# A down-projection by Strassen's seven products instead of eight block products

## The chip, the cores and the metric

The kernel runs on one core of one Trainium2 chip. The metric is the device time of one execution in microseconds. The core has five engines that work side by side, each with its own queue in a fixed order: TensorE (PE, matmuls into PSUM), VectorE (DVE) and GpSimd (POOL) for elementwise work, ScalarE (ACT) for activations and copies, and SyncE (SP), which here issues nearly all transfers. The kernel is written in Tile, which traces the program, lays out each engine's queue by a timeline of its own, and places the semaphores. Only blocks under `in_order` have the order of the named engines fixed by hand.

## The reference

One layer of a sequence model on x of 512 tokens by 1024 channels, all in float32: a token-mixing sublayer (two branches, merged and projected), then a gated MLP. The change is in the MLP, which is this, with D_FF = 2752 and ALPHA = 2 ** 0.25:

```python
x = layer_norm(ALPHA * x + merged @ w_out[l], ln1_g[l], ln1_b[l])
u = causal_dwconv(x @ w_up[l], f_conv_w[l], f_conv_b[l])      # width 3
u_gate, u_val = jnp.split(u, 2, -1)
x = layer_norm(ALPHA * x + (jax.nn.silu(u_gate) * u_val) @ w_down[l], ln2_g[l], ln2_b[l])
```

## The kernel before

**Products in three matmuls.** Every float32 operand is split into a high part H, rounded to the PE's `fp32r` format by a copy on ACT, and a low part L, the source minus H, on DVE. A product is then H·H + L·H + H·L: three matmuls of 128x128 stationary against 512 moving columns, added up in a PSUM bank.

**The weight stream.** The weights lie in HBM as a list of units, 128 partitions by 1024 numbers each (512 KB), in the order in which they are used (`unit_list`). `advance` (L132) loads a unit (L136) up to four ahead into one of three `raw` tiles, and splits it up to two ahead into one of three pairs `wH`, `wL` (L159, L165). The loads wait in SP's queue for a free `raw` tile, and the splits for a free pair.

**The MLP.** 21 full tiles of 128 features and one half tile of 64. For each full tile, `feature_major` multiplies the gate unit (UG) and the value unit (UV), 24 matmuls each, with features on the partitions and the 512 tokens along the columns. Then ACT and DVE apply the convolution's taps (L505, L507), SiLU (L1050), the product of gate and value (L1051), and the split into `fH` and `fL` (L1053, L1054). The half tiles of gate and value come together in one unit (UM), and their product is put as H on 64 partitions and as L on the other 64 of one tile, `fHm` (L1061 to L1066), so that two matmuls do the work of three.

**The residual.** x after the first LayerNorm went to HBM as `x1d` without its gamma and beta. While the MLP ends, SP loads gammas and betas (L914) and the eight half rows `x1r` (L1076), and DVE folds gamma and beta in, sixteen operations of 128x512 (L1077, L1078). Their tiles come free as the last up-projection reads the old inputs for the last time.

**The down-projection.** `wide_product` multiplies token-major: four token tiles of 128 by two halves of 512 output channels, in the eight PSUM banks at once. It goes through the units of `w_down` one after another, 24 matmuls a unit, `step` (L944). The last five units (half tile included) are multiplied bank by bank, so that the banks are done one after another and each token tile's residual sum (L1090), statistics (L1091), normalisation and store go on beside the next bank's matmuls. This end is in a fixed order on PE, DVE, ACT and POOL: the rsqrt of LayerNorm (L232) and the addition of the last beta (L1109) are on POOL, the shift and scale on ACT (L1115), the multiplication by gamma on DVE (L1108).

Of the kernel before, what the change touches and what calls it, by code (L numbers as in the profile page):

```python
# [87 lines left out]
def trunk(ctx, tc, x, wts, pcm, prow, out):  # L88
# [10 lines left out]
    def mm_bank(name):  # L99
        return pm.tile([P, 512], F32, tag="mm", name=name)  # L100
# [29 lines left out]
    EXTRA.update({u: ("ff", "xw", "xw", 4) for u in UX["DN"][-2:]})  # L130

    def advance(n, hl=HL_AHEAD):  # L132
        while st["raw"] <= min(n + RAW_AHEAD, len(UNITS) - 1):
# [5 lines left out]
        while st["hl"] <= min(n + hl, len(UNITS) - 1):  # L139
# [5 lines left out]
            if u == UX["DN"][-3]:  # L145
                hls[u] = [[tmp(f"w{q}{u}{i}", F32R) for i in range(2)] for q in "HL"]
                for i in range(2):
                    r_ = raw[:, 512 * i:512 * i + 512]
                    nc.scalar.copy(hls[u][0][i], r_)
                    nc.vector.tensor_tensor(hls[u][1][i], r_, hls[u][0][i].bitcast(F32), ALU.subtract)  # L150
                st["hl"] += 1
                continue
            H = pool.tile([P, 1024], F32R, tag=tH, name=f"wH{u}", bufs=nb_)
            L = pool.tile([P, 1024], F32R, tag=tL, name=f"wL{u}", bufs=nb_)
            if u == 0:
                nc.gpsimd.tensor_copy(H[:, 0:512], raw[:, 0:512])
                nc.scalar.copy(H[:, 512:], raw[:, 512:])
            else:
                nc.scalar.copy(H, raw)  # L159
            if u == len(UNITS) - 1:  # L160
                nc.gpsimd.memset(L[64:128, :].bitcast(F32), 0.0)
                nc.vector.tensor_tensor(L[0:64, :], raw[0:64, :], H[0:64, :].bitcast(F32), ALU.subtract)
            else:
                eng = nc.gpsimd if u == 0 else nc.vector
                eng.tensor_tensor(L, raw, H.bitcast(F32), ALU.subtract)  # L165
# [28 lines left out]
    def tmp(name, dt=F32, shape=(P, 512)):  # L194
        return tp.tile(list(shape), dt, tag="tmp", name=name)
# [865 lines left out]
    nc.scalar.activation(tg[0:64, :], tg[0:64, :], AF.Silu)  # L1061
    nc.scalar.copy(tv[0:64, :], tg[64:128, :])
    nc.vector.tensor_tensor(tg[0:64, :], tg[0:64, :], tv[0:64, :], ALU.mult)
    H = hpart("fHm")
    nc.scalar.copy(H[0:64, :], tg[0:64, :])
    nc.vector.tensor_tensor(H[64:128, :], tg[0:64, :], H[0:64, :].bitcast(F32), ALU.subtract)  # L1066
# [20 lines left out]
    def wd(c, hf):
        ps = wd_tail(c, hf)
        rr = x1r[c][hf]
        nc.vector.scalar_tensor_tensor(rr, rr, ALPHA, ps, ALU.mult, ALU.add)  # L1090
        nc.vector.bn_stats(bn2[c][:, hf, :], rr)  # L1091
        if hf == 1:
            ln_finish(bn2[c], mv2[:, c, :], rs2[:, c:c + 1], f"2_{c}")

    def store(c, hf, n0=0, n1=512):
        nc.sync.dma_start(out[c * P:(c + 1) * P, 512 * hf + n0:512 * hf + n1], x1r[c][hf][:, n0:n1])

    def shift(c):
        nb = cst.tile([P, 1], F32, tag="nb", name=f"nb2_{c}", bufs=4)
        nc.vector.scalar_tensor_tensor(nb, mv2[:, c, 0:1], -1.0, rs2[:, c:c + 1], ALU.mult, ALU.mult)  # L1100
        return nb

    with in_order(*CORE):
        for c in range(NC):
            wd(c, 0)
            if c > 0:
                for hf in range(2):
                    nc.vector.tensor_tensor(x1r[c - 1][hf], x1r[c - 1][hf], gt2[0][hf], ALU.mult)  # L1108
                    nc.gpsimd.tensor_tensor(x1r[c - 1][hf], x1r[c - 1][hf], gt2[1][hf], ALU.add)  # L1109
                    store(c - 1, hf)  # L1110
            wd(c, 1)
            nb = shift(c)
            if c < NC - 1:
                for hf in range(2):
                    nc.scalar.activation(x1r[c][hf], x1r[c][hf], AF.Identity, bias=nb, scale=rs2[:, c:c + 1])  # L1115
# [84 lines left out]
```

## Time and profile before

| what | value |
|---|---|
| median of 3 runs | 942.77 us (942.12 to 942.94) |
| the profiled execution | 942.7 us, of which the span is 941.0 us |
| PE busy | 924.0 us, 98% of the span |
| DVE busy | 555.0 us, 59% |
| ACT busy | 382.3 us, 41% |
| POOL busy | 66.0 us, 7% |
| up-projection | to 812.7 us |
| down-projection's matmuls | 812.7 to 931.8 us |
| end | 931.8 to 941.0 us |

A row of the groups gives line, engine, operation, the tile written and the tiles read, shapes and count; then busy time and the mean duration in ns; then idle time ahead of them and what ended it. A row of a timeline gives start and length in us, and in brackets the idle time of its engine just before and what released it. A row of the chain gives start and length of a piece of the sequence of waits that ended last. Matmuls overlap one another, so the length of one is more than the distance to the next.

### The profile page before, as it was taken

The numbers are of one execution on the slowest core, as the hardware profiler recorded it, in microseconds if no ns is written. First come the engines' busy times: TensorE is split into PE (matmuls) and PEld (weight loads), VectorE is DVE, ScalarE is ACT, GpSimd is POOL, SyncE is SP. The second block draws the span as 40 slices with busy tenths as digits, with TensorE's granted clock in tenths as the row PEclk, the third lists the DMA queues.
The fourth block names the chain that finished last, engine by engine and source line by source line (L and its number), as shares of the span: only waits on it lengthen the run. The fifth ranks groups of instructions, "written<-read, shape, count | busy, mean of one in ns | idle before, by whom it ended". The sixth has DMA issues, their size and how long they took to land.

```text
span 941.0 us, 11703 instructions
## 1 busy us (share of the span) xinstructions
PE 924.0 (98%) x4565; PEld 762.3 (81%) x4565; DVE 555.0 (59%) x916; ACT 382.3 (41%) x572; POOL 66.0 (7%) x81
## 2 busy tenths in 40 slices
PE   7999999999999999999999999999999999999996
PEld 4988888888877888888888888888888888878884
DVE  6685889873556465324339467666666556642246
ACT  4456456442664552234122235544444444332121
POOL 3000000211012510000000000000000000000005
PEclk8999999999999999999999999999999999999998
DMA  5334326453232432223334352222322322632212
GB/s 186 105 101 138 109 88 142 123 147 118 90 111 70 139 109 77 102 90 96 106 112 157 112 178 91 90 90 92 109 90 93 110 90 91 251 128 90 95 62 90
DMA packets 46311, 105.13 MB, mean 112 GB/s; under 512 B 4064, under 2 KB 21144, under 8 KB 46256
## 3 DMA queue, kind: packets, MB, share of 16 engines
q1 hardware_dynamic: 45456, 103.30, 34.0%
q0 software_dynamic: 512, 1.07, 0.4%
q8 instruction: 36, 0.59, 0.3%
q14 instruction: 19, 0.16, 0.1%
q10 hardware_dynamic: 288, 0.02, 0.0%
HBM read 100.08 MB, written 4.30 MB: 111 GB/s over the span
## 4 chain that ended last, share of the span: by engine, by line
PE 94%; DVE 2%; DMA 1%; issue 1%; POOL 0%; ACT 0%; DVEq 0%; ACTq 0%; POOLq 0%
PE u L185 23%; PE wd L944 10%; PE g L185 9%; PE z L185 5%; PE o L185 5%; PE v L575 5%; PE xs L185 5%; PE pb L185 5%; PE pa L185 5%; PE wo L944 4%; PE bc L185 4%; PE q L185 2%; PE k L185 2%; PE bc L335 1%; PE up L185 1%
## 5 line engine op out<-in xcount | busy, mean ns | idle before, releaser
L165 DVE TENSOR_TENSOR wL<-raw,wH 128x1024 fp32r<-128x1024 f32 x151 | 186.4, 1238 | 231.3 <-ACT wH L159 229.2
L159 ACT CAST wH<-raw 128x1024 fp32r<-128x1024 f32 x152 | 159.1, 1051 | 285.5 <-PE g L185 62.8
L185 PE MATMUL u<-x1H,wL 128*128 128x512 f32 x312 | 121.4, 389 | 0.0
L185 PE MATMUL u<-x1L,wH 128*128 128x512 f32 x312 | 121.4, 389 | 0.0
L185 PE MATMUL u<-x1H,wH 128*128 128x512 f32 x312 | 121.4, 389 | 0.0
L185 PEld LDWEIGHTS u<-x1H,wH 128*128 128x128 f32 x312 | 58.6, 188 | 12.1
L185 PEld LDWEIGHTS u<-x1H,wL 128*128 128x128 f32 x312 | 58.6, 188 | 12.0
L185 PEld LDWEIGHTS u<-x1L,wH 128*128 128x128 f32 x312 | 58.6, 188 | 11.8
L944 PE MATMUL wd<-wH,fH 128*128 128x512 f32 x168 | 65.5, 390 | 0.8 <-ACT wH L159 0.8
L944 PE MATMUL wd<-wH,fL 128*128 128x512 f32 x168 | 65.4, 389 | 0.0
L944 PE MATMUL wd<-wL,fH 128*128 128x512 f32 x168 | 63.9, 389 | 0.0
L185 PE MATMUL g<-xnH,wH 128*128 128x512 f32 x128 | 50.1, 392 | 0.0
L185 PE MATMUL g<-xnH,wL 128*128 128x512 f32 x128 | 49.8, 389 | 0.0
L185 PE MATMUL g<-xnL,wH 128*128 128x512 f32 x128 | 49.8, 389 | 0.0
L232 POOL TENSOR_TENSOR rs<-ve,mhalf 128x1 f32<-128x1 f32 x12 | 7.6, 629 | 555.8 <-DVE ve L256 555.5
L944 PEld LDWEIGHTS wd<-wH,fH 128*128 128x128 f32 x168 | 31.5, 188 | 7.7 <-ACT wH L159 1.2
L944 PEld LDWEIGHTS wd<-wH,fL 128*128 128x128 f32 x168 | 31.5, 188 | 6.6
L944 PEld LDWEIGHTS wd<-wL,fH 128*128 128x128 f32 x168 | 31.5, 188 | 6.5
L1053 ACT CAST fH<-cg 128x512 fp32r<-128x512 f32 x21 | 13.0, 620 | 53.0 <-DVE cg L1051 53.0
L507 DVE SCALAR_TENSOR_TENSOR cv<-u,par,cv 128x511 f32<-128x511 f32 (+1 forms) x40 | 29.8, 746 | 0.7
L1050 ACT ACTIVATE cg<-cg 128x512 f32<-128x512 f32 x21 | 13.3, 632 | 40.8 <-DVE cg L507 40.8
L507 DVE SCALAR_TENSOR_TENSOR cg<-u,par,cg 128x511 f32<-128x511 f32 (+1 forms) x38 | 28.4, 746 | 0.6
(326 smaller groups left out, 1972.2 us busy)
## 6 DMA issues: line engine op xcount, KB each, us to landing
raw<-in_wts_dram SPq DMA_DIRECT2D x154, 512.0 KB, 3.3
csb<-scr SPq DMA_DIRECT2D x8, 512.0 KB, 7.3
gt<-in_prow_dram SPq DMA_DIRECT2D x12, 256.0 KB, 4.7
xt<-in_x_dram SPq DMA_DIRECT2D x4, 512.0 KB, 6.5
rb<-scr SPq DMA_DIRECT2D x4, 512.0 KB, 5.5
res<-in_x_dram SPq DMA_DIRECT2D x4, 512.0 KB, 5.3
x1d<-res SPq DMA_DIRECT2D x4, 512.0 KB, 2.6
x1r<-x1d SPq DMA_DIRECT2D x8, 256.0 KB, 5.7
```

The costliest lines, as they stand in the source:

```text
L159: nc.scalar.copy(H, raw)
L165: eng.tensor_tensor(L, raw, H.bitcast(F32), ALU.subtract)
L185: nc.tensor.matmul(ps[:, t0:t1], w_[:, k, :], a_[k][:, t0:t1], start=i == 0, stop=i == 3 * KD - 1)
L232: nc.gpsimd.tensor_tensor(dst, var, epsl[:, :n], ALU.pow)
L335: nc.tensor.matmul(fb[u][:, t], w_[:, k, :], a_[k][:, t], start=n == 1, stop=n == 3 * KD)
L507: nc.vector.scalar_tensor_tensor(dst[:, d:], ps[:, 0:T - d], prm(ws[n - 1 - d], j)[rows], dst[:, d:], ALU.mult, ALU.add)
L575: nc.tensor.matmul(banks[c], a_[k][:, cs_], w_[:, kk, :], start=first and s == 0, stop=last and s == 2)
L944: nc.tensor.matmul(banks[c, hf], a_[:, cs_], w_, start=k == 0 and s == 0, stop=k == n - 1 and s == len(prs) - 1)
L1050: nc.scalar.activation(tg, tg, AF.Silu)
L1053: nc.scalar.copy(H, tg)
```

## The change

The first 20 feature tiles (2560 rows of `w_down`) are multiplied by Strassen's method in Winograd's form. The features A are cut into quarters, token half by tiles 0 to 9 and 10 to 19, and the weights B likewise, tiles 0 to 9 and 10 to 19 by halves of the output channels:

- S1 = A21 + A22, S2 = S1 - A11, S3 = A11 - A21, S4 = A12 - S2
- T1 = B12 - B11, T2 = B22 - T1, T3 = T2 - B11, T4 = T2 - B21
- seven products: 1 = A11·B11, 2 = A12·B21, 3 = S4·B22, 4 = A22·T4 (made with the other sign), 5 = S1·T1, 6 = S2·T2, 7 = S3·T3

Each product goes over ten feature tiles in five steps of two tiles, for two token tiles, 12 matmuls a step. The order is product 2, 1, 5, then 6 and 3 mixed, 7, and 4. Feature tile 20 and the half tile ("the rest") are multiplied as before, four quarters of ten matmuls each, and ahead of the products.

- The up-projection makes tile i and tile i + 10 one after the other (`UP_ORDER`). POOL adds S1, S2 and S3 for the pair, and the features are split into the parts that the products read directly.
- The stream of units ends with the two units of the rest (DR). The seven products have a stream of their own, 30 blocks of 512 KB: some quarters are loaded more than once.
- The weight sums are made in place, two operations a step for products 5, 6, 7 and 4, on POOL (in product 4 the second one on DVE). Then come the splits on ACT and DVE. Each of the 20 steps of products 5, 6, 7 and 3 also splits a tile of feature sums, and S4 takes one operation of POOL and one of DVE in each step of product 5.
- The results are added to the residual by DVE from PSUM, in several passes: eight scalings with the rest (or product 2) and fourteen additions.
- PE's order is fixed for the whole stage. The order of all four engines is fixed only at the end, where the last two steps of product 4 are made for token tile 2 and then for token tile 3.

The diff, cut to its core:

```diff
-    for j in range(21):
+UP_ORDER = [j for i in range(10) for j in (i, i + 10)] + [20]
+    for j in UP_ORDER:
         add("UG", "cols", "w_up", 128 * j)
         add("UV", "cols", "w_up", FF + 128 * j)
     add("UM", "mixed")
-    for k in range(21):
+    add("DR", "rows", "w_down", 128 * 20)
+    add("DR", "last")
+    for k in range(20):
         add("DN", "rows", "w_down", 128 * k)
-    add("DN", "last")
...
+    for i, j in enumerate(UP_ORDER):
+        tg = gated(i, j)
+        if j < 10:
+            low = tg
+            split(a11[j // 2][0][:, j % 2, :], a11[j // 2][1][:, j % 2, :], tg[:, 0:TH])
+        elif j < 20:
+            p, q = (j - 10) // 2, j % 2
+            split(a2[p][0][:, q, :], a2[p][1][:, q, :], tg)
+            s1, s2, s3 = (sums[p][:, n, q, :] for n in range(3))
+            nc.gpsimd.tensor_tensor(s1, low[:, TH:], tg[:, TH:], ALU.add)
+            nc.gpsimd.tensor_tensor(s2, s1, low[:, 0:TH], ALU.subtract)
+            nc.gpsimd.tensor_tensor(s3, low[:, 0:TH], low[:, TH:], ALU.subtract)
+        else:
+            split(fr[0], fr[1], tg)
...
+    LOAD = {2: (bY, 10, 0), 1: (bX, 0, 0), 5: (bZ, 0, 1), 6: (bX, 10, 1), 3: (bZ, None, None), 7: (bX, 0, 0), 4: (bW, 10, 0)}
+    SUM = {5: 0, 6: 1, 7: 2, 3: 0}
+    steps = ([(2, i) for i in range(5)] + [(1, i) for i in range(5)] + [(5, i) for i in range(5)]
+             + [(6, 0), (6, 1), (3, 0), (6, 2), (3, 1), (6, 3), (3, 2), (6, 4), (3, 3), (3, 4)]
+             + [(7, i) for i in range(5)] + [(4, i) for i in range(5)])
...
+    def split_step(p, i):
+        H = wp.tile([P, 2, 512], F32R, tag="wH", name=f"dnH{p}{i}")
+        L = wp.tile([P, 2, 512], F32R, tag="wL", name=f"dnL{p}{i}")
+        whl[p, i] = H, L
+        if p in (2, 3):
+            raw = blk[(6 if p == 3 else p), i]
+            split(H, L, raw)
+            return
+        for q in range(2):
+            t = tt[2 * i + q]
+            if p in (5, 6, 4):
+                eng = nc.vector if p == 4 and q else nc.gpsimd
+                eng.tensor_tensor(t, blk[p, i][:, q, :], t, ALU.subtract)
+            elif p == 7:
+                nc.gpsimd.tensor_tensor(blk[7, i][:, q, :], t, blk[7, i][:, q, :], ALU.subtract)
+        if p == 7:
+            split(H, L, blk[7, i])
+        else:
+            for q in range(2):
+                split(H[:, q, :], L[:, q, :], tt[2 * i + q])
+
+    def sum_step(p, i):
+        if p in (5, 6, 7, 3):
+            n = at_["srn"]
+            at_["srn"] += 1
+            H, L = sr[2 * (n % 2)], sr[2 * (n % 2) + 1]
+            split(H, L, sums[i][:, SUM[p], :, :])
+            shl[p, i] = H, L
+        if p == 5:
+            s4, a12 = sums[i][:, 0, :, :], [t[:, :, 0:TH].bitcast(F32) for t in a2[i]]
+            nc.gpsimd.tensor_tensor(s4, a12[0], sums[i][:, 1, :, :], ALU.subtract)
+            nc.vector.tensor_tensor(s4, s4, a12[1], ALU.add)
+
+    def ahead(n):
+        for what, f, m in (("load", load_step, n + 3), ("hl", split_step, n + 2), ("s", sum_step, n + 1)):
...
+    def product(p, i, ms=(0, 1)):
+        aH, aL = operand(p, i)
+        H, L = whl[p, i]
+        first = i == 0 and p in (1, 5, 4)
+        for q in range(2):
+            for m in ms:
+                for s_, (a_, w_) in enumerate(((aH, H), (aL, H), (aH, L))):
+                    nc.tensor.matmul(LOAD[p][0][m], a_[:, q, m * P:(m + 1) * P], w_[:, q, :],
...
+    def rest(bank, c0, hf, name):
+        for m in range(2):
...
+            prs = ((fr[0], H0), (fr[1], H0), (fr[0], L0), (fr[2], H1), (fr[2], L1))
...
+    with in_order(ET.PE):
+        rest(bY, 0, 0, "11")
+        rest(bW, 0, 1, "12")
+        scaled(bW, 0, 1)
+        rest(bZ, 2, 1, "22")
+        scaled(bZ, 2, 1)
+        rest(bX, 2, 0, "21")
+        scaled(bX, 2, 0)
+        for n, (p, i) in enumerate(steps[:-2]):
+            ahead(n)
+            product(p, i)
+            if (p, i) == (2, 4):
+                scaled(bY, 0, 0)
...
+            elif p == 7 and i < 2:
+                apply2(i)
+            elif (p, i) == (7, 4):
+                plus(bX, 2, 1)
+                plus(bX, 2, 0)
+                for c in (2, 3):
+                    nc.vector.bn_stats(bn2[c][:, 1, :], x1r[c][1])
+        ahead(len(steps) - 1)
     with in_order(*CORE):
+        for c in (2, 3):
+            for p, i in steps[-2:]:
+                product(p, i, (c - 2,))
+            plus(bW, 2, 0, (c - 2,))
+            nc.vector.bn_stats(bn2[c][:, 0, :], x1r[c][0])
+            ln_finish(bn2[c], mv2[:, c, :], rs2[:, c:c + 1], f"2_{c}")
+            if c == 2:
+                apply2(c)
+        nb = shift(c)
```

`split(H, L, t)` is the ACT copy into H and the DVE subtraction into L. `apply2(c)` is, for one token tile, the shift, two ACT passes, two DVE multiplications, two POOL additions and the stores. The pairs `wH`, `wL` keep their three buffers, and the residual's folds stay where they were in the program, behind the half tile's features and ahead of the down-projection.

More of the change, by code (lines that the diff above doesn't have):

```diff
@@ L129, in trunk @@
     EXTRA[UX["UG"][1]] = ("at", "bc", "bc", 3)
-    EXTRA.update({u: ("ff", "xw", "xw", 4) for u in UX["DN"][-2:]})
+    STREAM_END = UX["DR"][1]
     def advance(n, hl=HL_AHEAD):
-        while st["raw"] <= min(n + RAW_AHEAD, len(UNITS) - 1):
+        while st["raw"] <= min(n + RAW_AHEAD, STREAM_END):
             u = st["raw"]
@@ L1032, in trunk, with gated @@
     FM = [f"fmw{i}" for i in range(3)]
-    def hpart(name):
-        return ff.tile([P, T], F32R, tag="hT", name=name, bufs=43)
-    for j in range(21):
+    TH = T // 2
+    a11 = [[ff.tile([P, 2, TH], F32R, tag="a11", name=f"a11{q}{i}", bufs=10) for q in "HL"] for i in range(5)]
+    a2 = [[ff.tile([P, 2, T], F32R, tag="a2", name=f"a2{q}{i}", bufs=10) for q in "HL"] for i in range(5)]
+    sums = [ff.tile([P, 3, 2, TH], F32, tag="sum", name=f"sum{i}", bufs=5) for i in range(5)]
+    fr = [ff.tile([P, T], F32R, tag="fr", name=f"fr{i}", bufs=3) for i in range(3)]
+    def gated(i, j):
         pgv = []
-        for u in (UX["UG"][j], UX["UV"][j]):
+        for u in (UX["UG"][i], UX["UV"][i]):
             if u in up_banks:
@@ L1082, in trunk @@
     rs2 = cst.tile([P, NC], F32, name="rs2")
-    wd_tail = wide_product(UX["DN"], fH, fL, 5, "wd", last_stack=True)
     bn2 = [bn_tile(f"2_{c}") for c in range(NC)]
[L1087 to L1091, printed above, removed]
+    bX, bY = ([mm_bank(f"wd{n}{i}") for i in range(2)] for n in "xy")
+    bZ, bW = ([sm_bank(f"wd{n}{i}") for i in range(2)] for n in "zw")
@@ new lines, in trunk, with block @@
+    sr = [rp.tile([P, 2, TH], F32R, tag="r", name=f"sr{i}") for i in range(4)]
+    tt = [tmp(f"tt{k}") if k < 8 else ff.tile([P, 512], F32, tag="tt", name=f"tt{k}", bufs=2) for k in range(10)]
+    DN = UX["DN"]
+    def block(k0, hf, i):
+        return wts[DN[k0 + 2 * i]:DN[k0 + 2 * i] + 2, :, 512 * hf:512 * hf + 512].rearrange("u p c -> p u c")
+    LOAD = {2: (bY, 10, 0), 1: (bX, 0, 0), 5: (bZ, 0, 1), 6: (bX, 10, 1), 3: (bZ, None, None), 7: (bX, 0, 0), 4: (bW, 10, 0)}
+    SUM = {5: 0, 6: 1, 7: 2, 3: 0}
@@ new lines, in ahead, with operand @@
+    def ahead(n):
+        for what, f, m in (("load", load_step, n + 3), ("hl", split_step, n + 2), ("s", sum_step, n + 1)):
+            while at_[what] <= min(m, len(steps) - 1):
+                f(*steps[at_[what]])
+                at_[what] += 1
+    def operand(p, i):
+        if p == 1:
+            return [t for t in a11[i]]
+        if p in (2, 4):
+            o = TH * (p == 4)
+            return [t[:, :, o:o + TH] for t in a2[i]]
+        return shl[p, i]
+    def product(p, i, ms=(0, 1)):
+        aH, aL = operand(p, i)
+        H, L = whl[p, i]
+        first = i == 0 and p in (1, 5, 4)
+        for q in range(2):
+            for m in ms:
+                for s_, (a_, w_) in enumerate(((aH, H), (aL, H), (aH, L))):
+                    nc.tensor.matmul(LOAD[p][0][m], a_[:, q, m * P:(m + 1) * P], w_[:, q, :],
+                                     start=first and q == 0 and s_ == 0, stop=i == 4 and q == 1 and s_ == 2,
+                                     skip_group_check=True)
@@ new lines, in rest, with scaled @@
+    def rest(bank, c0, hf, name):
+        for m in range(2):
+            cs_ = slice((c0 + m) * P, (c0 + m + 1) * P)
+            ws = slice(512 * hf, 512 * hf + 512)
+            (H0, L0), (H1, L1) = (weights(u) for u in UX["DR"])
+            prs = ((fr[0], H0), (fr[1], H0), (fr[0], L0), (fr[2], H1), (fr[2], L1))
+            for s_, (a_, w_) in enumerate(prs):
+                nc.tensor.matmul(bank[m], a_[:, cs_], w_[:, ws], start=s_ == 0, stop=s_ == 4, skip_group_check=True)
+    def scaled(bank, c0, hf):
+        for m in range(2):
+            rr = x1r[c0 + m][hf]
+            nc.vector.scalar_tensor_tensor(rr, rr, ALPHA, bank[m], ALU.mult, ALU.add)
@@ L1092, in wd, with plus, stats2 @@
+    def plus(bank, c0, hf, ms=(0, 1)):
+        for m in ms:
+            rr = x1r[c0 + m][hf]
+            nc.vector.tensor_tensor(rr, rr, bank[m], ALU.add)
+    def stats2(c, hf):
+        nc.vector.bn_stats(bn2[c][:, hf, :], x1r[c][hf])
         if hf == 1:
@@ L1101, in shift, with apply2 @@
         return nb
-    with in_order(*CORE):
[L1104 to L1115, printed above, removed]
+    def apply2(c):
+        nb = shift(c)
+        for hf in range(2):
+            nc.scalar.activation(x1r[c][hf], x1r[c][hf], AF.Identity, bias=nb, scale=rs2[:, c:c + 1])
+        for hf in range(2):
+            nc.vector.tensor_tensor(x1r[c][hf], x1r[c][hf], gt2[0][hf], ALU.mult)
+            nc.gpsimd.tensor_tensor(x1r[c][hf], x1r[c][hf], gt2[1][hf], ALU.add)
+            store(c, hf)
@@ new lines, in trunk @@
+    with in_order(ET.PE):
[11 more added lines that the diff above has]
+                scaled(bY, 0, 0)
+            elif (p, i) == (1, 4):
+                plus(bX, 0, 0)
+                for c in range(2):
+                    stats2(c, 0)
+            elif (p, i) == (5, 4):
+                plus(bZ, 2, 1)
+            elif (p, i) == (6, 4):
+                plus(bX, 0, 1)
+            elif (p, i) == (3, 4):
+                plus(bZ, 0, 1)
+                for c in range(2):
+                    stats2(c, 1)
+            elif p == 7 and i < 2:
[6 more added lines that the diff above has]
+        ahead(len(steps) - 1)
```

45 lines of the change are left out of this document (25 added, 20 removed).

## The prediction, made before the changed kernel ran

> **What bounds the kernel now.** I read the page's engine shares first, then the windows by stage, the chain, the groups of the last stage, and the queues of single engines where the two stages meet.
>
> ```profile
> span 941.0 us, 11703 instructions
> ...
> PE 94%; DVE 2%; DMA 1%; issue 1%; POOL 0%; ACT 0%; DVEq 0%; ACTq 0%; POOLq 0%
> ```
>
> PE holds 94% of the chain that ended last. The windows (engine busy and instruction count, granted clock, DMA share) show the same for the stage that is changed:
>
> ```profile
> 812.70:931.60 118.90, 118.12 (x521) 97.33 (x519) 51.90 (x71) 27.83 (x31) 8.13 (x8) 1.00 0.34 118
> 931.60:941.00 9.40, 0.20 (x1) 0.00 (x0) 4.96 (x9) 0.60 (x1) 4.57 (x5) 0.75 0.30 112
> ```
>
> In the down-projection PE has no room, while VectorE (DVE) is busy 51.9 of 118.9 us, ScalarE (ACT) 27.8 and GpSimd (POOL) 8.1. Matmuls overlap, so their price is their step in the chain, not their duration in the groups:
>
> ```profile
> 829.95 98.70 PE wd L944 x434
> ```
>
> ```profile
> L944 PE MATMUL wd<-wH,fH 128*128 128x512 f32 x168 | 65.5, 390 | 0.8 <-ACT wH L159 0.8
> ...
> L165 DVE TENSOR_TENSOR wL<-raw,wH 128x1024 fp32r<-128x1024 f32 x36 | 43.9, 1225 | 79.8 <-ACT wH L159 79.8
> ...
> L1109 POOL TENSOR_TENSOR x1r<-x1r,gt 128x512 f32<-128x512 f32 x6 | 8.5, 1442 | 8.5 <-DVE x1r L1108 8.5
> ```
>
> 98.70 / 434 = 0.2274 us a matmul, though each lasts 0.390. PE waited once, 0.8 us, for a weight copy.
>
> **Matmuls removed.** Before: 21 full row tiles x 8 banks x 3, and 2 x 8 for the stacked half tile, 520. After: seven products x 5 steps x 2 tiles x 2 banks x 3 = 420, and the rest 4 quarters x 2 banks x 5 = 40, together 460. All keep 128x128 against 512 columns. 60 x 0.2274 = 13.6 us; the 0.8 us wait lies behind the new stalls below and goes too: **-14.4**. The chains that follow decide how much of it stays. (The up-projection stays as it was: the same matmuls in another order, PE full; its three POOL sums of 256 columns a pair fall in 10.9 us in which DVE is not full.)
>
> **A wait at the seam.** The rest's matmuls now come first, in a PE order that is fixed, and the fourth of them reads the half tile's features (`fr[2]`). Before, these were read only by the last stack, at the stage's end. How late were they made?
>
> ```profile
> 812.69 0.39 PE L944 MATMUL wd<-wH,fH 128*128 128x512 f32 x1
> ```
>
> ```profile
> 813.62 0.77 ACT L505 ACTIVATE cgm<-um,par 128x512 f32<-128x512 f32 x1
> 824.19 0.63 ACT L1061 ACTIVATE cgm<-cgm 64x512 f32<-64x512 f32 x1 [9.80 <-DVE cgm L507]
> 824.83 0.62 ACT L1062 COPY cvm<-cgm 64x512 f32<-64x512 f32 x1
> 828.33 0.62 ACT L1065 CAST fHm<-cgm 64x512 fp32r<-64x512 f32 x1 [2.88 <-DVE cgm L1063]
> ```
>
> ```profile
> 819.08 0.74 DVE L507 SCALAR_TENSOR_TENSOR cgm<-um,par,cgm 128x511 f32<-128x511 f32 x1
> ...
> 823.35 0.74 DVE L507 SCALAR_TENSOR_TENSOR cgm<-um,par,cgm 128x510 f32<-128x510 f32 x1
> ...
> 824.61 3.10 DVE L1078 TENSOR_TENSOR x1r<-x1r,gt 128x512 f32<-128x512 f32 x5
> 827.62 0.68 DVE L1063 TENSOR_TENSOR cgm<-cgm,cvm 64x512 f32<-64x512 f32 x1
> 828.98 0.69 DVE L1066 TENSOR_TENSOR fHm<-cgm,fHm 64x512 fp32r<-64x512 f32 x1 [0.69 <-ACT fHm L1065]
> 829.93 3.50 DVE L165 TENSOR_TENSOR wL<-raw,wH 128x1024 fp32r<-128x1024 f32 x3 [0.26 <-ACT wH L159]
> ```
>
> The reader sees one chain, ACT-DVE-DVE-ACT-ACT-DVE-ACT-DVE, strewn among the sixteen folds of the residual (L1077, L1078) in DVE's queue; it ends at 829.7. PE starts the stage at 812.7 and does three matmuls, to 813.4. If DVE's queue keeps its order, PE waits 829.7 - 813.4 = 16.3 us. If the chain ran through at once, its durations from 813.62 give 0.77 + 1.4 (two taps, which overlap a little) + 0.63 + 0.62 + 0.68 + 0.62 + 0.69, with hand-overs 819.2, and a wait of 5.8. I take the upper end, since these very instructions, next to the same folds, took that long: **+16.3** (5.8 to 16.3).
>
> A PE that has been idle comes back slowly. In these windows PE's engine alone is shown (busy, granted clock):
>
> ```profile
> 13.50:18.00 4.50, 4.50 (x18) 0.50 0.12 46
> 18.10:22.00 3.90, 3.90 (x24) 1.00 0.35 119
> 931.80:936.20 4.40, 0.01 (x1) 1.00 0.32 119
> 936.30:941.00 4.70, 0.00 (x0) 0.50 0.30 112
> ```
>
> After the last matmul the clock fell to half within 4.5 us, and at the start PE worked 4.5 us before it was full again. Half of 4.5: **+2.3** (0 to 3.4). The Trainium skill, "TensorE: Matmul & The Clock Gate", Part 1, has the clock back after one busy window of about 3.4 us; by that figure the estimate would be 1.7 and the sum 0.6 lower. The 4.5 us here are not against it, since its windows run free.
>
> So the rest's other 37 matmuls end at 829.7 + 8.4 + 2.3 = 840.4 and the seven products begin; by PE alone they would end 420 x 0.2274 = 95.5 later, at 935.9.
>
> **The shared work of DVE and POOL.** The change gives DVE and POOL many elementwise operations with two SBUF inputs: each split subtracts H from its source, and POOL forms the weight sums and the sum S4. What happens when both engines run such operations together? POOL's queue and DVE's, in two places:
>
> ```profile
> 171.95 1.65 POOL L677 TENSOR_TENSOR y<-y,yo 128x512 f32<-128x512 f32 x1 [5.38 <-DVE yo L676]
> 174.24 2.21 POOL L646 TENSOR_TENSOR xd<-xc,DE 128x1024 f32<-128x1024 f32 x1 [0.64 <-PE st L693]
> ```
>
> ```profile
> 172.38 2.29 DVE L165 TENSOR_TENSOR wL<-raw,wH 128x1024 fp32r<-128x1024 f32 x1
> 174.60 0.74 DVE L507 SCALAR_TENSOR_TENSOR kT<-k,par,kT 128x511 f32<-128x511 f32 x1
> ```
>
> ```profile
> 222.23 2.20 POOL L677 TENSOR_TENSOR y<-y,yo 128x512 f32<-128x512 f32 x1 [19.45 <-DVE yo L676]
> ```
>
> ```profile
> 222.07 1.22 DVE L165 TENSOR_TENSOR wL<-raw,wH 128x1024 fp32r<-128x1024 f32 x1
> ```
>
> The split that takes 1.22 took 2.29 when it met a POOL operation: POOL ended at 173.60, and the split 1.07 us after that. The other way round POOL, in DVE's way, took 2.20 instead of 1.65 and ended at 224.43, 1.14 us after the split's end at 223.29. They take turns; POOL's turn for 512 columns is 1.14 us. (An operation of DVE with one input in PSUM, the tap at 174.60, kept its usual 0.74 while POOL was at work.)
>
> [...]
>
> Now the turns, with DVE's steps of (3.10 - 0.68) / 4 = 0.605 us for 512 columns and (3.50 - 1.22) / 2 = 1.14 for 1024. POOL can begin when the first tile of product 1 is split, as it overwrites that tile in place. The split tiles have three buffers and two are held to the end of the rest, so product 1's first split waits for product 2's third step: 840.4 + 3 x 12 x 0.2274 + (0.62 + 0.69) = 849.9. From there:
> - DVE, 512 columns: product 1 nine, 5 twenty (four a step), 6 fifteen, 3 five, 7 five, 4 fifteen: 69 x 0.605 = 41.7. 1024 columns: products 3 and 7, 10 x 1.14 = 11.4.
> - POOL: weight sums 10 + 10 + 10 + 5 for products 5, 6, 7, 4, and five S4: 40 x 1.14 = 45.6.
> - The normalisation of the first two token tiles, 4 x 0.605 + 4 x 1.14 = 7.0.
>
> The sum is 105.7 us of turns, where PE alone leaves 935.9 - 4.1 - 849.9 = 81.9. The last split is then made at 955.6, and 18 matmuls follow (of the last two steps' 24 the first six need no more than the split before): 4.1 us, PE ends at 959.7, against 935.9: **+23.8**. I hide under it DVE's operations that read PSUM (12 additions, 6 statistics, 18 x 0.69 = 12.4 us), because POOL's turns are nearly half of the time and do not stop them. If nothing covered them, +12.4. Below: if POOL's turns cost DVE nothing, 0. ACT's copies, 3 x 0.62 at most in a step of 2.73 us, are not late. The stream's 30 loads of 512 KB are 15.7 MB in some 130 us, 121 GB/s, where the window of before has 118; on SP they stand behind the loads of gammas and residual, which the folds, ended at 827.7, had already received, and the first is needed at 840.4. Eight scalings of the residual (8 x 0.69) fall between the folds and 849.9, when DVE has but product 2's five splits to make. These three I cost at nothing; the range's upper end stands for them.
>
> **The tail.** The last two token tiles are finished together, and in one fixed order per engine. Before:
>
> ```profile
> 928.20 1.53 ACT L1115 ACTIVATE x1r<-x1r,nb,rs 128x512 f32<-128x512 f32 x2 [4.83 <-DVE nb L1100]
> ```
>
> ```profile
> 931.84 0.69 DVE L1090 SCALAR_TENSOR_TENSOR x1r<-x1r,wd 128x512 f32<-128x512 f32 x1 [0.56 <-PE wd L944]
> ...
> 934.35 0.16 DVE L1100 SCALAR_TENSOR_TENSOR nb<-mv,rs 128x1 f32<-128x1 f32 x1 [0.66 <-POOL rs L232]
> ```
>
> From the last matmul to `nb` takes 2.7 us. Tile 2's last matmul is 2.7 us before tile 3's, so tile 2's `nb` comes as PE ends. Then two ACT passes (1.53) and two DVE multiplications stand in DVE's queue ahead of tile 3's addition, to 2.2 us after PE's end, and POOL's two additions stand ahead of its rsqrt. **+2.5** (0 to 4).
>
> **The sum.** Against the profiled execution's 942.7 us (span 941.0 and 1.7 around it; the median of the runs is 942.77): 942.7 - 14.4 + 16.3 + 2.3 + 23.8 + 2.5 = 973.2; I forecast 973.
>
> **Rivals.**
> 1. *The seam's chain runs through*, since the rest now needs it early: wait 5.8, all later steps 10.5 earlier, 962.7. For it: nothing but the order of DVE's queue holds it up, and that order is made anew. Against: two taps of which the second waits for the first alone were 4.3 us apart.
> 2. *Turns don't overlap with anything*: the PSUM readers add 12.4, 985.6. For it: S4 makes DVE wait for POOL and POOL for DVE within one step.
> 3. *PE stays the bound* and POOL's work fits into DVE's gaps: 949.4 with the late chain. It decides from a turn of (81.9 - 55.5) / 44 = 0.60 us a POOL operation; the rows say 1.14.
> 4. *Faster*: the same bound with the seam's chain at its lower price. It is the seam that decides this one: PE as the bound wins from a wait under 9.6 us, and at 5.8 gives 938.9.
>
> The change's own count of matmuls is plain from its loops, so that it saves none is no rival.
>
> **Chances.** Forecast 0.38, rival 1 0.30, rival 2 0.13, rival 3 0.11, rival 4 0.08. The range 946 to 988 leaves out rival 4 and the ends of the outer cases. A measurement here tells about 0.2% (1.9 us) from no change: faster 0.07, same 0.03, slower 0.90.
>
> **What would show it.** Right: PE idle behind the third matmul of the rest, released by DVE on `fr`; from product 5 on, PE waiting for weight splits; DVE's splits stretched beyond 0.69 and 1.22 whenever POOL is busy; POOL at two thirds or more of that stretch. Wrong: PE without a gap from product 5 on, splits at their old durations beside a busy POOL, or the half tile's features ready before 820.

## The result and the profile after

The changed kernel takes 978.39 us (median of 4 runs, 976.17 to 979.14) against 942.86 us for the kernel before on the same chip: a ratio of 1.0374, interval 1.0356 to 1.0392. It is slower, 5.4 us above the forecast of 973 and inside its range. The profiled execution, the fastest of the four, took 976.2 us, 974.4 of them the span; all positions below are in that span.

In the rows, `fr` are the features of the rest (`fr[2]` the half tile's), `sr` the splits of feature sums, `dn` and `tt` the weight blocks, `dnH` and `dnL` their splits, and `wdx`, `wdy`, `wdz`, `wdw` the four pairs of PSUM banks.

The page of the changed kernel, in the lines that answer to those of before:

```profile
span 974.4 us, 11906 instructions
...
PE 920.7 (94%) x4505; PEld 754.0 (77%) x4505; DVE 633.1 (65%) x994; ACT 408.3 (42%) x626; POOL 159.4 (16%) x151
...
PE 87%; DVE 7%; issue 2%; DMA 2%; POOL 1%; ACT 1%; DVEq 0%; ACTq 0%; POOLq 0%
```

The 60 matmuls are gone (4565 before, 4505 now), and PE's share of the chain fell from 94% to 87%: DVE now carries 7% of it. The windows of the changed kernel show where (PE, weight load, DVE, ACT, POOL, each busy us and count; then granted clock, DMA share, GB/s):

```profile
600.00:807.20 207.20, 207.20 (x915) 171.55 (x914) 128.13 (x156) 89.03 (x117) 26.78 (x31) 1.00 0.31 102
...
812.70:960.00 147.30, 110.47 (x446) 86.96 (x446) 127.23 (x141) 53.59 (x83) 73.99 (x46) 0.90 0.35 122
```

The up-projection lost nothing: PE is busy 207.2 of 207.2 us, with POOL's new sums beside it. In the down-projection PE worked 118.1 of 118.9 us before; now, up to 960, it works 110.5 of 147.3, while DVE has 127.2 and POOL 74.0. PE waits in two places. The waits of PE's queue from 790 on (us in total, times, longest):

```profile
PE wdy L1203 <- DVE fr L1082: 17.4, 1, 17.4
PE wdx L1192 <- DVE sr L1058: 11.4, 9, 3.6
PE wdz L1192 <- DVE sr L1058: 8.1, 2, 6.6
```

The first is the seam: the half tile's features. The other eleven all wait for the splits of the feature sums (`sr`), which stand in DVE's queue behind the splits of the weights. The groups of the last stage show why DVE is late:

```profile
L1058 DVE TENSOR_TENSOR dnL<-tt,dnH 128x512 fp32r<-128x512 f32 x40 | 44.7, 1164 | 3.6 <-ACT dnH L1057 3.6
L1150 POOL TENSOR_TENSOR tt<-dn,tt 128x512 f32<-128x512 f32 x25 | 41.7, 1690 | 32.1 <-DVE dnL L1058 20.3 <-DMA dn<-in_wts_dram 11.6
...
L1058 DVE TENSOR_TENSOR sr<-sum,sr 128x512 fp32r<-128x512 f32 x20 | 20.5, 1027 | 0.0
...
L1213 DVE TENSOR_TENSOR x1r<-x1r,wdx 128x512 f32<-128x512 f32 x8 | 5.1, 677 | 0.5 <-PE wdx L1192 0.5
```

A weight split of 512 columns takes 1164 ns on average and a split of sums 1027, where 690 was the length in the kernel before. These are means of two kinds: a split that met a sum of POOL's for its whole length took 1.74 to 1.78 us, one that met none 0.68. The addition from PSUM (L1213), of the same size but with one input in SBUF, keeps its 677. DVE's queue and then POOL's, in the stretch where both work without a gap:

```profile
855.03 15.98 DVE L1058 TENSOR_TENSOR dnL<-tt,dnH 128x512 fp32r<-128x512 f32 x10
```

```profile
853.39 20.03 POOL L1150 TENSOR_TENSOR tt<-dn,tt 128x512 f32<-128x512 f32 x12 [0.63 <-DVE dnL L1058]
```

The second of the ten splits starts 0.60 us after the first, and from there on they start 1.70 apart, as POOL's sums do: the two engines alternate, one operation each. A split's step of 0.605 leaves 1.10 us for POOL's turn. A sum that began with no such operation in its way took this long:

```profile
874.04 1.26 POOL L1150 TENSOR_TENSOR tt<-dn,tt 128x512 f32<-128x512 f32 x1 [0.63 <-DVE dnL L1058]
```

### The profile page after: what moved, and what is told of

Its sections match the earlier page's. It is cut to its first block, busy times and chain, and to the rows that moved or that the text cites. A ratio compares the mean times of both kernels' runs of the same rounds, so it can differ in the third digit from the quotient of the medians.

```text
span 974.4 us, 11906 instructions
## 1 busy us (share of the span) xinstructions
PE 920.7 (94%) x4505; PEld 754.0 (77%) x4505; DVE 633.1 (65%) x994; ACT 408.3 (42%) x626; POOL 159.4 (16%) x151
## 4 chain that ended last, share of the span: by engine, by line
PE 87%; DVE 7%; issue 2%; DMA 2%; POOL 1%; ACT 1%; DVEq 0%; ACTq 0%; POOLq 0%
PE u L182 22%; PE g L182 9%; PE z L182 5%; PE o L182 5%; PE v L572 5%; PE xs L182 4%; PE pa L182 4%; PE pb L182 4%; PE wo L941 4%; PE bc L182 3%; DVE dnL L1058 3%; PE q L182 2%; PE k L182 2%; PE wdx L1192 2%; PE wdy L1192 1%
## 5 line engine op out<-in xcount | busy, mean ns | idle before, releaser
L162 DVE TENSOR_TENSOR wL<-raw,wH 128x1024 fp32r<-128x1024 f32 x132 | 163.4, 1241 | 180.7 <-ACT wH L156 178.7
L156 ACT CAST wH<-raw 128x1024 fp32r<-128x1024 f32 x133 | 139.3, 1050 | 233.5 <-PE g L182 62.8
L1058 DVE TENSOR_TENSOR dnL<-tt,dnH 128x512 fp32r<-128x512 f32 x40 | 44.7, 1164 | 3.6 <-ACT dnH L1057 3.6
L1150 POOL TENSOR_TENSOR tt<-dn,tt 128x512 f32<-128x512 f32 x25 | 41.7, 1690 | 32.1 <-DVE dnL L1058 20.3
L1057 ACT CAST dnH<-tt 128x512 fp32r<-128x512 f32 x40 | 22.8, 618 | 41.4 <-PE wdz L1192 13.6
L1192 PE MATMUL wdx<-dnH,sr 128*128 128x512 f32 x80 | 29.1, 428 | 11.4 <-DVE sr L1058 11.4
L1192 PE MATMUL wdz<-dnH,sr 128*128 128x512 f32 x80 | 26.8, 414 | 8.1 <-DVE sr L1058 8.1
L1192 PEld LDWEIGHTS wdx<-dnH,sr 128*128 128x128 f32 x80 | 16.1, 202 | 18.9 <-DVE sr L1058 15.5
L1057 ACT CAST dnH<-dn 128x1024 fp32r<-128x1024 f32 x15 | 15.7, 1052 | 35.0 <-issue 11.2
L504 DVE SCALAR_TENSOR_TENSOR cv<-u,par,cv 128x511 f32<-128x511 f32 (+1 forms) x40 | 29.8, 746 | 0.7
L504 DVE SCALAR_TENSOR_TENSOR cg<-u,par,cg 128x511 f32<-128x511 f32 (+1 forms) x38 | 28.3, 746 | 0.6
```

Of the source, the lines that this page charges most:

```text
L504: nc.vector.scalar_tensor_tensor(dst[:, d:], ps[:, 0:T - d], prm(ws[n - 1 - d], j)[rows], dst[:, d:], ALU.mult, ALU.add)
L1057: nc.scalar.copy(H, t)
L1058: nc.vector.tensor_tensor(L, t, H.bitcast(F32), ALU.subtract)
L1150: eng.tensor_tensor(t, blk[p, i][:, q, :], t, ALU.subtract)
L1192: nc.tensor.matmul(LOAD[p][0][m], a_[:, q, m * P:(m + 1) * P], w_[:, q, :], start=first and q == 0 and s_ == 0, stop=i == 4 and q == 1 and ...
```

## The experiments

The kernel before, run beside them, took 942.75 us (experiments 1 to 4), 942.59 (5 to 8) and 942.72 (9 and 10). The theory: at the seam PE waits for the half tile's chain in DVE's queue, and in the products for DVE, because POOL's operations with SBUF inputs take turns with DVE's. The rivals are in each expectation.

**1. The half tile's chain first.** The order of DVE's queue is fixed by hand from the half tile's taps to the residual's folds.

```diff
+    with in_order(ET.DVE):
+        conv_taps(tg, pg, FM, "fmb", 0)
...
+                nc.vector.tensor_tensor(t, t, gt1[1][hf], ALU.add)
```

> DVE's order is fixed over the half tile's chain and the residual's folds, so that the chain stands ahead of the folds. My theory: the wait of 17.4 us at the seam falls to about 6 (the chain's own length), and since the seven products are paced by DVE and POOL only from product 1's splits on, everything behind shifts by the same 11 us: about 967 us against 978. Rival (DVE's total work from the first fold on sets the end, and the wait at the seam only hides some of it): the wait falls, the end stays at 974 to 979.

Measured 970.98 us (970.27 to 971.39), ratio 1.0298 (1.0283 to 1.0313). PE's waits in this kernel:

```profile
PE wdx L1193 <- DVE sr L1058: 13.5, 9, 3.8
PE wdz L1193 <- DVE sr L1058: 9.1, 3, 7.3
PE wdy L1204 <- DVE fr L1083: 6.1, 1, 6.1
```

The wait at the seam fell as expected, from 17.4 to 6.1, by 11.3; the time fell by only 7.4. The waits behind it grew from 19.5 to 22.6: DVE still has to do the folds, now while PE is already in the products. The time lies between theory and rival.

**2. The half tile's matmuls later.** The sixteen matmuls that need `fr[2]`, and the scalings of the residual, come after product 2, and the quarters go in the order bX, bZ, bW, bY (the pairs of banks `wdx`, `wdz`, `wdw`, `wdy`).

```diff
-            prs = ((fr[0], H0), (fr[1], H0), (fr[0], L0), (fr[2], H1), (fr[2], L1))
+            prs = ((fr[2], H1), (fr[2], L1)) if half else ((fr[0], H0), (fr[1], H0), (fr[0], L0))
...
             if (p, i) == (2, 4):
-                scaled(bY, 0, 0)
+                for b_ in quarters:
+                    rest(*b_, True)
+                    scaled(*b_)
```

> The half tile's sixteen matmuls are made after product 2, with the scalings of the residual. My theory: no wait of more than 2 us is left at the seam and product 1 starts at about 835 in place of 854; POOL's sums can begin some 20 us earlier, but DVE has folds, chain and product 2's splits to do until about 838, so the end comes 11 to 23 us earlier: 955 to 967 us. Rival (DVE's total work sets the end): 974 to 979.

Measured 972.10 us (971.04 to 974.93), ratio 1.0307 (1.029 to 1.0324): between the theory's range and the rival's. PE's waits:

```profile
PE wdx L1192 <- DVE sr L1058: 12.8, 8, 3.8
PE wdz L1192 <- DVE sr L1058: 8.6, 2, 7.3
PE wdy L1203 <- DVE cgm L504: 6.3, 1, 6.3
PE wdy L1192 <- DVE dnL L1058: 1.9, 1, 1.9
```

The wait for `fr` is gone, and two others stand in its place that I had not seen. The fourth pair of banks (`wdy`) held the half tile's up-projection, and is free only when the second tap (L504), between the folds in DVE's queue, has read it. And product 2's splits stand behind the folds. What the seam costs is DVE's queue, not one operand.

**3. POOL writes and doesn't read.** Each of POOL's 40 operations in the stage becomes two fills of the same tiles.

```diff
-                eng.tensor_tensor(t, blk[p, i][:, q, :], t, ALU.subtract)
+                if eng is nc.vector:
+                    eng.tensor_tensor(t, blk[p, i][:, q, :], t, ALU.subtract)
+                else:
+                    eng.memset(blk[p, i][:, q, :], 0.5)
+                    eng.memset(t, 0.25)
```

> Each of POOL's forty sums (35 weight sums, five S4) is replaced by two memsets of 128x512, which write and do not read: the sums are left out, the instructions that wait for them stay. POOL stays at about 1.1 us for each. My theory (the two engines take turns because both read two SBUF operands): DVE's splits fall from 1.16 to about 0.69 us and from 1.50 to 1.23, PE has next to no wait from product 5 on, and the end comes about 27 us earlier: 949 to 953 us. Rival (POOL's own time, or the chain DVE to POOL to DVE within a step, sets the pace): the splits may become shorter, but PE still waits for the sums and the time stays above 970.

Measured 955.50 us (954.82 to 956.29), ratio 1.0135 (1.012 to 1.015), 22.9 us less than the changed kernel. The groups of the stage, and PE's waits:

```profile
L1058 DVE TENSOR_TENSOR dnL<-tt,dnH 128x512 fp32r<-128x512 f32 x40 | 27.0, 711 | 11.3 <-ACT dnH L1057 11.2
...
L1058 DVE TENSOR_TENSOR sr<-sum,sr 128x512 fp32r<-128x512 f32 x20 | 13.7, 684 | 0.0
...
L1154 POOL MEMSET tt<- 128x512 f32 x25 | 12.9, 524 | 6.8 <-DVE dnL L1058 6.2
```

```profile
PE wdy L1209 <- DVE fr L1082: 17.2, 1, 17.2
PE wdx L1198 <- DVE sr L1058: 2.3, 3, 1.0
```

With POOL at work on the same tiles at the same places, but only writing, DVE's splits are back at 711 and 684 ns, and of 19.5 us of waits in the products 2.3 are left. It is POOL's reading that DVE pays for: 38 of the stage's 75 splits ran beside a fill for more than 0.3 us, and none of them was stretched. With the same number of operations DVE's busy time fell by 33.3 us. The engine shares of the changed kernel again, then of this one:

```profile
PE 920.7 (94%) x4505; PEld 754.0 (77%) x4505; DVE 633.1 (65%) x994; ACT 408.3 (42%) x626; POOL 159.4 (16%) x151
PE 915.4 (96%) x4505; PEld 751.5 (79%) x4505; DVE 599.8 (63%) x994; ACT 408.2 (43%) x626; POOL 137.4 (14%) x191
```

The time is 2.5 us above the theory's upper end. Two fills (1.05 us) are also shorter than a sum (1.26 alone), so this run does not price POOL's own length, in the chain from sum to copy to split, apart from its reading.

**4. DVE does POOL's sums itself.** All 40 operations go to DVE.

```diff
-                eng = nc.vector if p == 4 and q else nc.gpsimd
+                eng = nc.vector
...
-            nc.gpsimd.tensor_tensor(s4, a12[0], sums[i][:, 1, :, :], ALU.subtract)
+            nc.vector.tensor_tensor(s4, a12[0], sums[i][:, 1, :, :], ALU.subtract)
```

> All forty sums are made by DVE; POOL has only the rsqrt and the additions of the last beta. My theory: an operation of POOL costs DVE 1.1 us of its turn, one of DVE's own 0.6, so the work gets shorter: about 88 us of DVE from 850 on up to product 7's last split in place of 97, a few stretched operations less, and the time falls to 955 to 965 us. Rival (DVE is the bound because it has too much to do, and POOL relieves it): 24 us more work on DVE, 990 to 1002 us.

Measured 963.53 us (962.76 to 963.96), ratio 1.0219 (1.0204 to 1.0234): 14.9 us less, though DVE has 40 operations more. Two groups, and the engine shares:

```profile
L1058 DVE TENSOR_TENSOR dnL<-tt,dnH 128x512 fp32r<-128x512 f32 x40 | 27.6, 724 | 2.0 <-ACT dnH L1057 2.0
...
L1150 DVE TENSOR_TENSOR tt<-dn,tt 128x512 f32<-128x512 f32 x30 | 19.4, 680 | 0.9 <-DMA dn<-in_wts_dram 0.9
```

```profile
PE 917.5 (95%) x4505; PEld 751.4 (78%) x4505; DVE 623.3 (65%) x1034; ACT 408.4 (42%) x626; POOL 95.3 (10%) x111
```

40 sums of 0.605 us are 24.2 us if DVE makes them; POOL's cost DVE 33.3 by experiment 3, or 0.83 each, since not every one met a two-input operation of DVE. DVE's busy time falls by 9.8 us, from 633.1 to 623.3, and the time by 14.9. Of the difference, 4.7 us can be the half clock behind PE's two long waits in the changed kernel (below); here no wait in the products is longer than 1.4 us and the clock stays full. The run rules out the rival that DVE has no room for the sums.

**5. Both, the chain first and the sums on DVE.** The edits of 1 and 4 together.

> The half tile's chain ahead of the folds and all sums on DVE. With the chain first alone the wait at the seam fell by 11.3 us and the time by 7.4. With the sums on DVE, DVE was busy 90.0 of 98.0 us behind the seam, and idle 6 of the 10 us of the rest. My theory now (DVE's work from the first fold on is the bound, and the wait at the seam costs only what DVE idles in it): about 6 us less than 963.5, 956 to 960. Rival (PE's waits add up): 11 us less, 952. Second rival (DVE has no slack left): no change.

Measured 954.30 us (954.01 to 954.55), ratio 1.0125 (1.0111 to 1.0139). That is below the theory's range and above the rival's 952. Against experiment 4, the seam's wait fell from 17.9 to 6.1 and the time by 9.2 us. With a less loaded DVE, more of the seam's gain comes through than in experiment 1 (9.2 of 11.8 against 7.4 of 11.3); the rest still goes to the products.

**6. The folds early.** The residual's sixteen folds are made in the up-projection, where DVE has room, and the result goes through HBM a second time; the sums are on DVE.

```diff
+        if 4 <= i < 12:
+            fold((i - 4) // 4, i % 4)
...
-            nc.sync.dma_start(t, x1d[:, c, 512 * hf:512 * hf + 512])
-            nc.vector.tensor_tensor(t, t, gt1[0][hf], ALU.mult)
-            nc.vector.tensor_tensor(t, t, gt1[1][hf], ALU.add)
+            nc.sync.dma_start(t, x1f[:, c, 512 * hf:512 * hf + 512])
```

> All sums on DVE, and the sixteen folds of the residual moved into the up-projection, where DVE is busy 129 of 207 us and PE does not wait for it: the residual is loaded, folded and stored again there. My theory (DVE's work at the seam and behind it is the bound): 9.6 us of DVE fall away where they count and the half tile's chain is through by about 820; 946 to 950 us. Rival (PE's wait at the seam alone counts): the same as with the chain first, 952 to 960. If the up-projection is slowed by the folds, its PE shows waits.

Measured 951.91 us (951.64 to 952.66), ratio 1.0101 (1.0086 to 1.0117), 11.6 less than experiment 4, 1.9 above the theory's upper end and at the rival's lower one. PE still waits 7.4 us at the seam, where operations of S4 now stand in the chain, and 8.4 in the products. Against experiment 5 the seam's wait is 1.3 longer and the time 2.4 shorter, which speaks against a wait at the seam that counts alone.

**7. The folds early, the sums on POOL.** The edit of 6 without that of 4.

> The folds moved into the up-projection as in the run before, but the sums stay on POOL as in the changed kernel. My theory (the turns of DVE and POOL set the pace from product 1's first split on, and that comes earlier by what falls away at the seam): 964 to 968 us. The difference to the same kernel with the sums on DVE is the price of the turns with no wait at the seam: 15 us or more. Rival (the turns only cost what DVE lacks in time; with 9.6 us less work they fit): less than 955.

Measured 969.09 us (967.79 to 970.62), ratio 1.0282 (1.0268 to 1.0296). It is 1.1 above the theory's range; PE waits 20.5 us in the products. Against experiment 6 the only difference is the engine of the 40 sums: the sums on POOL cost 17.2 us (969.09 - 951.91), also without the folds in the way.

**8. All of it.** Sums on DVE, folds early, the half tile's matmuls after product 2, and tile 3's statistics ahead of tile 2's multiplication by gamma at the end.

> Sums on DVE, folds in the up-projection, the half tile's matmuls behind product 2, and at the end tile 3's statistics ahead of tile 2's multiplications by gamma. By my theory PE starts the products at about 819 and would end alone at 918; DVE has some 107 us of work from 814 on, so that the products end at 922 to 927, and the tail is 10 us: 936 to 943 us, so about even with the kernel before. Rival (some wait takes the place of those removed): 946 or more.

Measured 946.72 us (945.63 to 947.41), ratio 1.0044 (1.0031 to 1.0056): better than every version so far, and still slower than before. It missed the theory's range and lies in the rival's. PE now goes from the up-projection into the products without a wait; the first of them begins at 818.0. Two windows of this kernel:

```profile
835.00:850.00 15.00, 15.00 (x68) 12.43 (x67) 15.00 (x26) 5.94 (x11) 0.00 (x0) 1.00 0.38 128
850.00:865.00 15.00, 11.66 (x49) 8.67 (x48) 15.00 (x26) 7.29 (x14) 0.00 (x0) 1.00 0.11 35
```

DVE works 15.0 of 15.0 us; in the second window PE gets only 11.7. PE's waits in the products are 9.9 us in all. The change of order at the end showed no gain: 12.6 us from PE's last matmul, where the changed kernel had 11.3.

**9. Less for DVE.** As 8, but S4 is made by POOL in the up-projection (a fourth sum beside S1 to S3), the last additions of token tiles 0 and 1 are on DVE, and the end is as in the change.

```diff
-            nc.gpsimd.tensor_tensor(s4, a12[0], sums[i][:, 1, :, :], ALU.subtract)
-            nc.vector.tensor_tensor(s4, s4, a12[1], ALU.add)
...
+            nc.gpsimd.tensor_tensor(s4, tg[:, 0:TH], s2, ALU.subtract)
...
-            nc.gpsimd.tensor_tensor(x1r[c][hf], x1r[c][hf], gt2[1][hf], ALU.add)
+            (nc.vector if c < 2 else nc.gpsimd).tensor_tensor(x1r[c][hf], x1r[c][hf], gt2[1][hf], ALU.add)
```

> Sums on DVE, folds early and the half tile late, as in the version at 946.7 (there DVE was busy without a gap from 835 to 865 and from 895 to 925, and PE waited 9.9 us). Here DVE is relieved further: S4 is made in the up-projection by POOL (one operation of 256 columns a tile, into 10 KB that constants of the token mixing gave up), so that ten of DVE's operations leave product 5 (10 x 0.605 = 6.1 us), and tile 0's and 1's last additions go from POOL to DVE, at 0.605 in place of a turn of 1.14 each (2.1 us). The end is in after's own order again (11.3 us in place of 12.6). If DVE is the bound: 940 to 945, and no PE wait left in product 5. If something else holds PE there (the blocks' loads, the clock): 946 to 948.

Measured 945.82 us (945.08 to 946.26), ratio 1.0033 (1.002 to 1.0045), just above the theory's end. The same window as above and a later one:

```profile
850.00:865.00 15.00, 12.63 (x55) 9.80 (x54) 15.00 (x26) 6.14 (x11) 0.00 (x0) 1.00 0.14 48
...
895.00:910.00 15.00, 12.25 (x49) 8.94 (x50) 15.00 (x25) 5.92 (x9) 0.09 (x1) 1.00 0.52 176
```

Even without S4, product 5 gives DVE five operations a step, two sums and three splits, 5 x 0.605 = 3.0 us against PE's 2.73. DVE stays full in these stretches, and PE still waits 7.6 us.

Part of the gain is hidden by a loss elsewhere. From the start of the down-projection to the end this version takes 128.8 us where experiment 8 took 133.5, but it starts at 814.6 and not at 812.2. The time is lost where the two branches are merged: from 457.6 to 480.0 PE makes 97 matmuls here and 100 in experiment 8, busy throughout at full clock in both. The edit moved constants to another place in SBUF; whether that is the cause was not tested. Without the 2.4 us the time would be about 943.4, an estimate, and inside the theory's range.

**10. Without the weight sums.** As 9, with these operations of DVE's taken out.

> The same, with the 35 weight sums on DVE left out (products 5, 6, 7 and 4 multiply with the blocks as they are; every load, split and matmul stays). 35 x 0.605 = 21 us of DVE go. If DVE alone held the products back, PE runs from 818.0 without a wait: 436 matmuls x 0.2274 = 99.1, to 917.1, and with 11.3 of tail and 1.7 around the span 930 to 934. If the stream of blocks or ACT's copies are a second bound just below DVE: 936 to 942, with PE waiting for a copy that waits for a block.

Measured 939.76 us (938.21 to 940.18), ratio 0.9966 (0.9952 to 0.9979), in the rival's range, but not for the rival's reason. From 820 to 895 PE now runs without a gap. Then it waits three times, 3.8 us in all. The longest wait in PE's queue, DVE's queue, and the windows:

```profile
908.70 0.58 PE L1196 MATMUL wdx<-dnH,sr 128*128 128x512 f32 x1 [2.47 <-DVE sr L1058]
```

```profile
905.56 0.68 DVE L1238 TENSOR_TENSOR x1r<-x1r,gt 128x512 f32<-128x512 f32 x1
906.16 0.68 DVE L1058 TENSOR_TENSOR dnL<-tt,dnH 128x512 fp32r<-128x512 f32 x1
906.76 0.68 DVE L1239 TENSOR_TENSOR x1r<-x1r,gt 128x512 f32<-128x512 f32 x1
907.36 0.68 DVE L1058 TENSOR_TENSOR dnL<-tt,dnH 128x512 fp32r<-128x512 f32 x1
907.97 0.68 DVE L1058 TENSOR_TENSOR sr<-sum,sr 128x512 fp32r<-128x512 f32 x1
```

```profile
906.00:909.00 3.00, 0.53 (x2) 0.30 (x2) 3.00 (x6) 0.71 (x2) 0.00 (x0) 1.00 0.47 176
909.00:912.00 3.00, 3.00 (x8) 2.30 (x7) 1.45 (x3) 0.00 (x0) 0.00 (x0) 0.50 0.24 89
```

The normalisation of the first two token tiles (L1238, L1239) stands in DVE's queue ahead of the split that product 7 needs, and PE, having waited 2.47 us, comes back at half clock. So 21 us less work for DVE brings 6.1 us, and the kernel is then only 3.0 us faster than before. The late start of the stage costs this version 2.4 us too, and is part of why it misses 930 to 934.

## Why the prediction held, and where its terms were off

The terms of the sum against the profiled execution of the change, which is 33.4 us longer in span:

| step | predicted | measured |
|---|---|---|
| 60 matmuls and a wait of 0.8 removed | -14.4 | -14.4, and 0.9 more by an earlier start of the stage |
| wait at the seam | +16.3 | +17.9 |
| half clock after it | +2.3 | +1.5 |
| products against PE alone | +23.8 | +27.2 |
| tail | +2.5 | +2.1 |

**The seam.** Right in place and cause. The forecast put the products' start at 840.4, and they start at 840.3. That it fits so well is in part luck. The chain of waits of the changed kernel:

```profile
840.43 13.60 PE wdy L1192 x60
...
944.94 1.69 DVE sr L1058
946.67 2.82 PE wdx L1192 x11
949.49 10.89 PE wdw L1192 x48
```

The half tile's chain kept its place in DVE's queue. Its last operation, in DVE's timeline, met the first S4 of POOL's; then PE's queue at the seam:

```profile
828.67 1.59 DVE L1082 TENSOR_TENSOR fr<-cgm,fr 64x512 fp32r<-64x512 f32 x1
```

```profile
811.75 0.94 PE L1203 MATMUL wdy<-wH,fr 128*128 128x512 f32 x2
812.53 0.40 PE L1203 MATMUL wdy<-wL,fr 128*128 128x512 f32 x1
830.31 0.79 PE L1203 MATMUL wdy<-wH,fr 128*128 128x512 f32 x1 [17.38 <-DVE fr L1082]
```

The operation took 1.59 where 0.69 was its length, so the chain ended 0.6 us later than forecast, at 830.3. PE came 0.9 us earlier, at 811.75; it gained these 0.9 in the first 25 us of the program, in a stage that the change does not touch. Counted as the forecast did, from where the fourth matmul would have started (812.4), the wait is 17.9, which is 1.6 more than forecast. The other 37 matmuls took 9.96 us in place of 8.41, 1.5 more and not 2.3. The earlier start, the longer wait and the shorter half clock cancel to 0.1.

What the forecast had wrong here is that it summed the seam as a cost of its own. Rival 1 expected 10.5 us from an early chain; experiments 1 and 5 took 11.3 and 11.8 off this wait and got 7.4 and 9.2. While PE waits at the seam, DVE works off what the products would otherwise wait for: in both places the late queue is DVE's.

**The turns of DVE and POOL** are shown to be the main cost. By taking POOL's reads away, experiment 3 gained 22.9 us, where the term said 23.8; experiments 4, 6 and 7 showed that the kernel gains 14.9 to 17.2 if DVE does POOL's work itself. The Trainium skill, "SBUF — State Buffer", section "Who interferes with whom", says that a DVE instruction with two SBUF inputs contends with a GpSimd instruction that reads SBUF and not with one that only writes. The trace agrees on both halves: 1.74 to 1.78 us for a split beside POOL's sums, 0.68 to 0.69 beside its fills. For DVE's two-port modes the same section of the Trainium skill states a hold for the whole instruction. These operations show a little less than that: a pair took 1.70 us, where 0.605 and the 1.26 of an unhindered POOL sum would be 1.87. The forecast's 1.14 for POOL's turn is close to the 1.10 of the steady stretch, and rival 2, with nothing overlapped, did not come.

The term itself, 23.8 against 27.2, can be followed in DVE's queue. From POOL's first sum at 849.8 to the last split, ended at 959.0, it took 109.2 us, where the forecast had 105.7. By the lengths of its instructions in the trace, an estimate, DVE's own operations with two SBUF inputs are 52.5 us of that (forecast 55.5), POOL's turns 33.1 (50.2), the readers of PSUM and the statistics 12.1 (hidden under the turns), very small operations 2.0 (0) and idle time 9.5 (0). The hiding held: turns and readers together are 45.2 and not more than 50.2. What the forecast had left out is the idle time. For 8.5 us of it DVE waited for ACT's copies of the weights (seven waits), which the forecast had called not late and costed at nothing. The total came near in part by luck: the idle time left out (9.5) stands against turns and own operations put 8.0 us too high (5.0 and 3.0).

In PE's queue the 27.2 are 19.5 of waits, and twice PE came back at half clock, which the forecast had counted only at the seam:

```profile
879.85 0.79 PE L1192 MATMUL wdz<-dnH,sr 128*128 128x512 f32 x1 [6.55 <-DVE sr L1058]
...
884.65 0.63 PE L1192 MATMUL wdz<-dnH,sr 128*128 128x512 f32 x2
```

From 879.85 to 884.65 there are eleven matmuls, 4.8 us in place of 11 x 0.2274 = 2.5: 2.3 lost, at a granted clock of 0.54 from 880 to 885. After the wait of 3.6 us that ends at 939.82 the next eleven take 4.9 us, 2.4 lost. The remaining 3.0 us of the 27.2 are spread over the eleven restarts: each wait is counted from the end of a matmul, 0.16 us after the next one could have started (0.39 - 0.2274), and behind the nine shorter waits the first matmul takes 0.33 us in place of 0.2274.

**The signs named beforehand.** Right: PE idle behind the third matmul of the rest for `fr`, the stretched splits, and POOL at work for two thirds of the stretch from its first sum to the last split that PE waited for, by the window:

```profile
849.80:946.60 96.80, 77.43 (x308) 59.94 (x306) 87.35 (x89) 41.06 (x64) 66.93 (x42) 0.93 0.29 97
```

POOL has 66.9 of 96.8 us. Wrong in detail: PE waited not for the weight splits but for the sums' splits behind them, and the last one it waited for was product 7's at 946.6. The forecast had PE wait for product 4's last split, at 955.6, with 18 matmuls behind it. That split was made by 959.0, but PE did not wait for it: the last 71 matmuls ran without a wait. PE ended at 963.1, 3.4 us after the forecast's 959.7. So that step's total was near, while its picture of the last steps was not.

**Where the 13.6 us went.** They are in the trace, but PE is no longer the bound when they are saved: in experiments 8 and 9, with all sums kept, DVE is full in the stretches where PE waits longest. The best of these is 945.82, 0.33% above before, and some 2.4 of its 3.1 us over before are lost ahead of the down-projection. Not tried: moving the normalisation of token tiles 0 and 1 behind the products, and splitting more of the sums in the up-projection. Experiment 10 makes it unlikely that this brings much, since even without the 21 us of weight sums the time was only 3.0 us below before, or about 5.4 without the late start of the stage; that stays an inference.

## What to carry to other kernels

Matmuls removed by sums of operands are paid for in elementwise work; price that work by its engine and per step of the product (here 3.0 us of DVE against 2.73 of PE) before counting the matmuls. POOL is no second DVE for operations on two SBUF inputs: look in the trace for a place where both engines run them together, and compare POOL's turn with what DVE would need itself. When one engine's queue is late, shortening one wait for it moves the wait elsewhere: ask what else stands in that queue.

## What the runs showed of the hardware that was not expected

- Where both had work without a gap (855 to 871), DVE's splits and POOL's sums of 512 columns alternated, one operation each, at 1.70 us a pair: 0.605 for the split and 1.10 for POOL's turn.
- A fill of 128x512 on POOL takes 0.524 us and leaves DVE's two-input operations at 684 to 711 ns.
- PE's clock fell again inside a stage that was busy before and after. Waits of 3.6 and 6.6 us in the change were followed by some eleven matmuls at half clock, 2.4 and 2.3 us lost, and a wait of 2.5 us in experiment 10 by eight. The longest wait of experiment 9 in the products, 2.4 us, was not, so these runs give no fixed length of wait.
